# An offset of its own for every raw weight tile inside the area of cut weights

## The chip, the cores and the metric

The kernel runs on one core of one Trainium2 chip. The metric is the device time of one execution in microseconds (us). A difference of about 2% is what a measurement of this kernel is taken to tell from no change. The profiler records one execution: every instruction of the engines PE (matrix multiplies; its loads of the stationary operand are listed apart as PEld), ACT, DVE, POOL, and the queue engine SP, which issues the DMAs here.

## The reference

A bidirectional encoder trunk of two layers over 512 tokens of width 1024, all in float32. Each layer has four sub-layers:

```
for l in range(DEPTH):                                   # DEPTH = 2
    h = swiglu(rms_norm(x, norm_pre[l, 0]), ffn1_gate[l], ffn1_up[l], ffn1_down[l])   # 1024 -> 2816 -> 1024
    x = x + 0.5 * rms_norm(h, norm_post[l, 0])
    h = parallel_head_groups(rms_norm(x, norm_pre[l, 1]), ..., w_in[l], ..., w_out[l])
    x = x + rms_norm(h, norm_post[l, 1])
    h = memory_cross_attention(rms_norm(x, norm_pre[l, 2]), rms_norm(mem, mem_norm[l]), ...)
    x = x + rms_norm(h, norm_post[l, 2])
    h = swiglu(rms_norm(x, norm_pre[l, 3]), ffn2_gate[l], ffn2_up[l], ffn2_down[l])
    x = x + 0.5 * rms_norm(h, norm_post[l, 3])
```

`swiglu(u)` is `(silu(u @ w_gate) * (u @ w_up)) @ w_down`. Nearly all of the arithmetic is activations times weights that are read once from device memory.

## The kernel before

**Weights in two halves.** A float32 product is made of three products in the faster format fp32r: the weight W is cut into H (W rounded to fp32r) and L (W minus H), the activation likewise, and H·h, H·l and L·h are summed in PSUM (`mm3`, `mm3s`). So every weight goes through a pipeline of four steps, run by the class `Stream`:

1. `loader`: a DMA of 1 MB brings a raw tile (128 partitions x 2048 values) into one of two raw buffers (`RAW_BUFS`).
2. `cutter`: the raw tile is cut into chunks. ACT writes H of a chunk (a copy with rounding), DVE writes L (a subtraction). The chunks are cut strictly one after the other.
3. PE uses a chunk in its matrix multiplies.
4. `free`: after the last of them the chunk's place may be written again.

**The area of cut weights.** The chunks lie in one tile `wts` of 12,288 values (48 KB) in each partition. In the built program it starts at byte 36,800 of the partition, which is 64 bytes past a multiple of 128. A chunk of kind p or s takes 2048 values (1024 of H, then 1024 of L), a chunk of kind h takes half of that. `places` lists six places for p, at 0, 2048, ..., 10,240; five for s and one for h, which were all shifted by `SHIFT` = 16 values (64 bytes), so that s and h chunks begin at a multiple of 128 bytes. A place is taken if the bytes it covers meet no chunk that is alive (`where`), and goes to the end of its list when it is taken (`take`). Three extra chunk pairs (`wHx`, `wLx`) exist only during the transitions between sub-layers.

**Three ways of using a chunk.**

- *Plain columns* (kind c, chunks of kind p): the gate and up weights of the feed-forward layer that comes first and two column blocks of each later one, and the projections of the mixers and the attention. The chunk is the stationary operand (128 columns, 512 bytes in a row per load), the activations `uH`/`uL` stream past, 512 columns at a time (256 for the memory keys and for the first group of a sub-layer).
- *Rows* (two chunks of kind p per raw tile): `ffn_down`, `w_out`, `xattn_o`. Here the activation is stationary and the chunk streams past, 512 columns at a time. One raw tile is 48 matrix multiplies.
- *The fast form* (kind s): in three of the four feed-forward layers (`FAST`) the gate and up products are made in `gates_fast` by a Strassen-like scheme with 7 products instead of 8. DVE forms sums of weight blocks in a scratch tile `T`. One raw tile gives four chunks (three of kind s, one of kind h), used in 7 products of 12 matrix multiplies each, 84 in all, with 256 streaming columns and the chunk as the stationary operand. The products take the chunks in the order 0, 1, 0, 2, 1, 3, 3: chunk 0 is free after product 3, chunk 2 after 4, chunk 1 after 5, chunk 3 after 7. There are 54 such raw tiles, 18 in each of the three layers.

**Order.** The instructions are not written out in order: threads (the stream of weights, the cutter, evacuations of PSUM) offer operations, and `Sched` picks the next by a cost table of its own and by priorities. Where the cutter may take a place decides when its operations are offered, and so the order on ACT, DVE, SP and PE.

Of the kernel before, what the change touches and what calls it, by code (L numbers as in the profile page):

```python
# [21 lines left out]
KF = DFF // P  # L22
# [5 lines left out]
HL_BUFS = 6  # L28
# [58 lines left out]
class Op:  # L87


    def __init__(self, eng, calls, rd, wr, cost):  # L90
        self.eng, self.calls, self.rd, self.wr, self.cost = eng, calls, rd, wr, cost
        self.ready, self.size = 0.0, 0
        self.table = TABLE.get(calls[0][2].get("func")) if eng == "ACT" else None
# [267 lines left out]
class Stream:  # L361
# [6 lines left out]
    def __init__(self, k):  # L368
        self.k = k
        self.raws, self.parts, self.loaded, self.chunks = [], [], {}, {}  # L370
        self.cut = self.taken = 0
        self.limit = self.slack = 0
        self.extra = []
        self.T = None

    def open(self, raw, w):
        self.rawring = Ring(raw)
        self.w, self.live = w, set()
        self.places = {"p": [(2048 * i, 1024) for i in range(HL_BUFS)],
                       "s": [(2048 * i + self.SHIFT, 1024) for i in range(HL_BUFS - 1)],  # L380
                       "h": [(2048 * (HL_BUFS - 1) + self.SHIFT, 512)]}

    def add(self, ap, a, b, kind):
        self.parts += [(len(self.raws), j) for j in range(4 if kind == "s" else 2)]
        self.raws.append((ap, a, b, kind))

    def cols(self, w, c0, kind="c"):
        self.add(w[:, c0:c0 + 256].rearrange("(k p) c -> p k c", p=P), KD, 256, kind)
# [18 lines left out]
    def where(self, c):  # L407

        if self.extra and c < self.limit:
            return self.extra  # L410
        i, j = self.parts[c]
        kind = "p" if self.raws[i][3] != "s" else "h" if j == 2 else "s"
        for pl in self.places[kind]:
            if all(pl[0] + 2 * pl[1] <= lo or lo + 2 * n <= pl[0] for lo, n in self.live):
                return kind, pl
        return None

    def take(self, c):
        ch, got = Chunk(), self.where(c)
        if got is self.extra:  # L420
            ch.home, ch.slot = got, got.pop(0)
            return ch, ch.slot
        kind, pl = got
        self.places[kind].remove(pl)
        self.places[kind].append(pl)
        self.live.add(pl)
        ch.home, ch.slot = None, pl
        lo, n = pl
        return ch, (self.w[:, lo:lo + n], self.w[:, lo + n:lo + 2 * n])
# [54 lines left out]
class Kernel:  # L484
# [29 lines left out]
    def plan(self):  # L514

        A, st = self.D, self.st
        for l, i in self.subs:
            self.marks.append(len(st.parts))
            if i in (0, 3):
                g, u, d = (A[f"ffn{1 if i == 0 else 2}_{n}"][l] for n in ("gate", "up", "down"))  # L520
                for j in range(0, DFF, 256):
                    kind = "s" if (l, i) in FAST and j >= 256 * FAST[l, i] else "c"
                    st.cols(g, j, kind)
                    st.cols(u, j, kind)
                for k in range(0, DFF, 256):
                    st.rows(d, k)
            elif i == 1:
                w = A["w_in"][l]
                for c in (2560, 2048, 2816, 2304, 3072, 3328):
                    st.cols(w, c)  # L530
                st.block(w, 0, 1024)
                st.block(w, 512, 1024)
                for c in (0, 512, 256, 768, 1536, 1792, 3584, 3840):
                    st.cols(w, c)
                for k in range(0, D, 256):
                    st.rows(A["w_out"][l], k)
            else:
                q, k, v = (A[f"xattn_{n}"][l] for n in "qkv")
                for w, c in XORDER:
                    w = {"q": q, "k": k, "v": v}[w]  # L540
                    if w is v:
                        st.block(v, 0, c)
                        st.block(v, 512, c)
                    else:
                        st.cols(w, c)
                for k in range(0, D, 256):
                    st.rows(A["xattn_o"][l], k)
        self.marks.append(len(st.parts))


    def pool(self, name, **kw):
# [1393 lines left out]
```

## Time and profile before

| | us |
|---|---|
| median of 2 runs (2463.9 and 2466.07) | 2464.99 |
| the profiled execution, its own time | 2457.15 |
| its span, first to last instruction | 2455.4 |
| PE busy | 2406.9 (98%) |
| DVE busy | 1640.3 (67%) |
| ACT busy | 1108.3 (45%) |

The profiled execution is 7.8 us shorter than the median. Operands are named by tile: `ps<-uH,wts` is a multiply of `uH` with a chunk of `wts` into PSUM; `wts<-raw` and `wts<-T` are the cuts. A matrix multiply's recorded duration overlaps the next one's, so the pace of a stretch is its length over the number of multiplies that start in it.

### The profile page before, as it was taken

Reading aid. Unit: us, or ns where it says so; the run is one execution under the profiler, and the core shown is the slowest. Engines: PE = TensorE matmul, PEld = TensorE weight load, DVE = VectorE, ACT = ScalarE, POOL = GpSimd, SP = SyncE. Lnnn points to the kernel's source line nnn. Section 1 sums busy time; section 2 is a strip of 40 time slices with the busy share of each in tenths; the row PEclk is TensorE's granted clock in tenths of the full one; section 3 lists DMA queues with packets and bytes.
Section 4 is the critical chain, followed back from the end, with each engine's and each line's share of the span. In section 5 each row is a group of like instructions: output and inputs, shape, how many; then the busy total and the mean of one; then the engine's idle time right before and its main releaser. Section 6 shows DMA issues by size and latency. Waiting matters only on the chain. (4 is left out here: it accounts for less than half of the span.)

```text
span 2455.4 us, 37218 instructions
## 1 busy us (share of the span) xinstructions
PE 2406.9 (98%) x14990; PEld 2123.0 (86%) x14990; DVE 1640.3 (67%) x2560; ACT 1108.3 (45%) x1859; POOL 231.7 (9%) x696
## 2 busy tenths in 40 slices
PE   8999999999999999999999999998999999999998
PEld 7888888778889889998889998887888898899987
DVE  5582437768766568886378885485776665888852
ACT  4522425742444544555235554366424454455631
POOL 1000002331020020000010000125010200100001
PEclk9999999999999999999999999999999999999999
DMA  6632432355334322334213334234543243133340
GB/s 203 201 112 90 143 93 95 91 168 173 98 121 142 118 86 69 112 109 175 86 35 104 105 120 162 78 101 115 183 152 126 94 163 103 35 104 106 119 146 34
DMA packets 231202, 286.79 MB, mean 117 GB/s; under 512 B 29630, under 2 KB 190966, under 8 KB 231030
## 3 DMA queue, kind: packets, MB, share of 16 engines
q1 hardware_dynamic: 229878, 280.23, 35.3%
q10 hardware_dynamic: 1152, 4.19, 0.4%
q8 instruction: 117, 1.92, 0.3%
q14 instruction: 55, 0.45, 0.1%
HBM read 255.00 MB, written 29.39 MB: 116 GB/s over the span
## 5 line engine op out<-in xcount | busy, mean ns | idle before, releaser
L235 PE MATMUL ps<-uH,wts 128*128 128x256 f32 (+1 forms) x4064 | 994.1, 329 | 1.7 <-ACT sg L235 1.7
L235 PEld LDWEIGHTS ps<-uH,wts 128*128 128x128 f32 x4064 | 695.5, 188 | 71.1 <-ACT sg L235 1.9
L235 PE MATMUL ps<-uL,wts 128*128 128x256 f32 (+1 forms) x2032 | 665.8, 328 | 0.6 <-DVE uL L235 0.6
L235 DVE TENSOR_TENSOR wts<-raw,wts 128x1024 fp32r<-128x1024 f32 (+1 forms) x363 | 411.9, 1142 | 189.5 <-ACT wts L235 189.4
L235 ACT ACTIVATE wts<-raw 128x1024 fp32r<-128x1024 f32 (+1 forms) x363 | 357.3, 991 | 247.5 <-PE ps L235 163.0
L235 PEld LDWEIGHTS ps<-uL,wts 128*128 128x128 f32 x2032 | 386.4, 190 | 34.8 <-DVE uL L235 1.5
L235 PE MATMUL ps<-wts,uH 128*128 128x512 f32 x1152 | 363.7, 397 | 0.0
L235 PEld LDWEIGHTS ps<-wts,uH 128*128 128x128 f32 x1152 | 218.2, 191 | 44.5
L235 PE MATMUL ps<-wts,uL 128*128 128x512 f32 x576 | 227.0, 394 | 0.0
L235 ACT ACTIVATE sg<-ps 128x256 f32<-128x256 f32 (+1 forms) x196 | 93.3, 478 | 290.8 <-PE ps L235 290.7
L235 DVE TENSOR_TENSOR wts<-T,wts 128x1024 fp32r<-128x1024 f32 x108 | 132.3, 1225 | 49.2 <-ACT wts L235 48.5
L235 ACT ACTIVATE wts<-T 128x1024 fp32r<-128x1024 f32 x108 | 114.2, 1058 | 54.4 <-DVE T L235 54.4
L235 PEld LDWEIGHTS ps<-wts,uL 128*128 128x128 f32 x576 | 109.7, 191 | 23.4
L235 DVE TENSOR_TENSOR uL<-h,uH 128x512 fp32r<-128x512 f32 x76 | 51.5, 701 | 104.6 <-ACT uH L235 104.6
L235 POOL TENSOR_SCALAR sm<-sm 128x1 f32<-128x1 f32 (+1 forms) x165 | 39.2, 238 | 853.4 <-ACT junk L235 828.1
L235 ACT ACTIVATE uH<-h 128x512 fp32r<-128x512 f32 x76 | 45.6, 627 | 127.4 <-PE ps L235 123.7
L235 POOL TENSOR_SCALAR wpost<-wpost 128x1024 f32<-128x1024 f32 x4 | 15.4, 3853 | 919.1 <-DMA wpost<-in_norm_post_dram 679.8
L235 ACT ACTIVATE junk<-ps 128x512 bf16<-128x512 f32 (+1 forms) x96 | 47.1, 490 | 116.6 <-PE ps L235 102.2
L235 PE MATMUL ps<-wHx,uH 128*128 128x512 f32 x224 | 87.6, 391 | 0.0
L235 PE MATMUL ps<-wHx,uL 128*128 128x512 f32 x224 | 87.3, 390 | 0.0
L235 PE MATMUL ps<-wLx,uH 128*128 128x512 f32 x224 | 87.2, 389 | 0.0
L235 PE MATMUL ps<-s3H,wts 128*128 128x256 f32 x432 | 84.9, 281 | 0.0
(336 smaller groups left out, 4235.1 us busy)
## 6 DMA issues: line engine op xcount, KB each, us to landing
raw<-in_ffn_up_dram SPq DMA_DIRECT2D x44, 1024.0 KB, 5.1
raw<-in_ffn_down_dram SPq DMA_DIRECT2D x44, 1024.0 KB, 5.0
raw<-in_ffn_gate_dram SPq DMA_DIRECT2D x43, 1024.0 KB, 5.1
raw<-in_w_in_dram SPq DMA_DIRECT2D x32, 1024.0 KB, 6.1
raw<-in_w_out_dram SPq DMA_DIRECT2D x8, 1024.0 KB, 6.0
raw<-in_xattn_q_dram SPq DMA_DIRECT2D x8, 1024.0 KB, 5.3
raw<-in_xattn_k_dram SPq DMA_DIRECT2D x8, 1024.0 KB, 5.2
raw<-in_xattn_v_dram SPq DMA_DIRECT2D x8, 1024.0 KB, 5.1
```

The lines of the kernel that those rows point to most:

```text
L235: fn(*a, **kw)
```

## The change

Each raw tile gets a shift of its own, in values of 4 bytes, by which all of its chunks lie further on in the area. The 64-byte shift of the s and h places goes out of the list of places and into the shifts' default.

```diff
-                       "s": [(2048 * i + self.SHIFT, 1024) for i in range(HL_BUFS - 1)],
-                       "h": [(2048 * (HL_BUFS - 1) + self.SHIFT, 512)]}
+                       "s": [(2048 * i, 1024) for i in range(HL_BUFS - 1)],
+                       "h": [(2048 * (HL_BUFS - 1), 512)]}
...
+        self.shifts.append(self.SHIFT if kind == "s" else 0)
...
-        for pl in self.places[kind]:
-            if all(pl[0] + 2 * pl[1] <= lo or lo + 2 * n <= pl[0] for lo, n in self.live):
-                return kind, pl
+        for q in self.places[kind]:
+            pl = (q[0] + self.shifts[i], q[1])
+            if pl[0] + 2 * pl[1] <= 2048 * HL_BUFS and all(pl[0] + 2 * pl[1] <= lo or lo + 2 * n <= pl[0] for lo, n in self.live):
+                return kind, q, pl
...
+        fast = [i for i, r in enumerate(st.raws) if r[3] == "s"]
+        cols = [i for i, r in enumerate(st.raws) if 4 <= i < KF]
+        rows = [i for i, r in enumerate(st.raws) if r[1] == 2]
+        fine = list(range(1, 16))
+        for some, sh in ((fast, [0] + fine + [16 * k + d for k in range(1, 8) for d in (0, 4, 8, 12)] + [144, 160, 192, 224, 256, 320, 384, 448, 512, 640]),
+                         (cols, fine[::2] + [24, 32, 48, 64, 72, 80, 96, 112, 116, 120]),
+                         (rows, fine + [16 * k + d for k in range(1, 8) for d in (0, 4, 8, 12)])):
+            for i, e in zip(some, sh):
+                st.shifts[i] = e
```

All 54 fast raw tiles get a shift from the list: 0; 1 to 15; every fourth value from 16 to 124; and ten from 144 to 640. Counted from the start of the partition, a shift of 16 (and of 48, 80, 112, 144) starts a tile at a multiple of 128 bytes, as all fast tiles did before; 13 of the others (0 among them) start at an odd multiple of 64 bytes, 36 at no multiple of 64 bytes. 18 plain column tiles of the first feed-forward layer get shifts of 1 to 120 (the first eight of them odd), and the first 43 row tiles get 1 to 15 and every fourth value from 16 to 124, of which 36 are no multiple of 16 values; a chunk that the cutter puts into an extra pair takes no shift, so 52 row chunks are shifted inside the area, 43 of them by no multiple of 16 values. All other tiles lie where they lay.

Each instruction is still there, with the same shape and the same count on every engine. Two things besides the addresses are different. A chunk with a shift covers the end of its place and the beginning of the next one, so it shuts out a chunk with another shift from that neighbour; and a p chunk with a shift no longer fits in the sixth place, which ends with the area. In the fast form, three to five chunks were alive when a new one was placed, now three or four. And since the cutter takes places at other moments, the order on the engines differs.

On DVE, in the middle of the second fast layer, the work on one raw tile stood like this before (`T<-raw` forms the sums, the `wts` rows write L, `sg` and `h` are the evacuation of finished products):

```order
L235 TENSOR_TENSOR T_10296<-raw_83 128x2x512 [waits DMAHW7_49,DVE_49]
L235 TENSOR_TENSOR T_10296<-raw_83,T_10296 128x512 [waits DVE_49]
L235 TENSOR_TENSOR wts<-raw_83,wts 128x1024 [waits Activation_49]
L235 TENSOR_TENSOR wts<-T_10296,wts 128x1024 [waits PE_49,Activation_49]
L235 TENSOR_TENSOR wts<-raw_83,wts 128x512 [waits PE_49,Activation_49]
L235 TENSOR_TENSOR T_10296<-raw_83,T_10296 128x512 [waits DVE_49]
L235 TENSOR_TENSOR sg_10299<-ps_76,sg_10299 128x512
L235 TENSOR_TENSOR sg_10299<-ps_77,sg_10299 128x512 [waits PE_49]
L235 TENSOR_TENSOR wts<-T_10296,wts 128x1024 [waits Activation_49]
```

The same raw tile now:

```order
L235 TENSOR_TENSOR T_10296<-raw_83 128x2x512 [waits DMAHW7_49,DVE_49]
L235 TENSOR_TENSOR T_10296<-raw_83,T_10296 128x512 [waits DVE_49]
L235 TENSOR_TENSOR wts<-raw_83,wts 128x1024 [waits PE_49,Activation_49]
L235 TENSOR_TENSOR h_10284<-sg_10299,sg_10297 128x512
L235 TENSOR_TENSOR wts<-T_10296,wts 128x1024 [waits PE_49,Activation_49]
L235 TENSOR_TENSOR sg_10298<-ps_81,sg_10298 128x512 [waits Activation_49]
L235 TENSOR_TENSOR wts<-raw_83,wts 128x512 [waits Activation_49]
L235 TENSOR_TENSOR T_10296<-raw_83,T_10296 128x512 [waits DVE_49]
L235 TENSOR_TENSOR sg_10298<-ps_78,sg_10298 128x512 [waits PE_49]
L235 TENSOR_TENSOR wts<-T_10296,wts 128x1024 [waits Activation_49]
```

The L of chunk 0 now waits for PE as well as for ACT, since its place is that of the raw tile before, and evacuations have moved in between the cuts of chunks 0, 1 and 2.

On ACT, at the same place, before (from the copy of PSUM that follows the raw tile's first two products):

```order
L235 ACTIVATE sg_10299<-ps_76 128x512 [waits PE_49]
L235 ACTIVATE wts<-T_10296 128x1024 [waits DVE_49]
L235 ACTIVATE wts<-raw_83 128x1024 [waits DMAHW7_49]
L235 ACTIVATE sg_10299<-ps_76 128x256 [waits PE_49]
L235 ACTIVATE wts<-T_10296 128x1024 [waits DVE_49,Activation_49]
L235 ACTIVATE sg_10299<-ps_76 128x256 [waits PE_49]
L235 ACTIVATE wts<-raw_83 128x512 [waits Activation_49]
```

And now:

```order
L235 ACTIVATE wts<-T_10296 128x1024 [waits DVE_49]
L235 ACTIVATE sg_10298<-ps_81 128x512 [waits PE_49]
L235 ACTIVATE wts<-raw_83 128x1024 [waits DMAHW7_49]
L235 ACTIVATE sg_10298<-ps_81 128x256 [waits PE_49]
L235 ACTIVATE wts<-T_10296 128x1024 [waits DVE_49,Activation_49]
L235 ACTIVATE sg_10298<-ps_81 128x256 [waits PE_49]
L235 ACTIVATE wts<-raw_83 128x512 [waits Activation_49]
```

Here only the H of the previous raw tile's last chunk has moved ahead of the first copy of PSUM; the H of chunk 0 still follows that copy, and the H of chunk 1 the second one.

More of the change, by code (lines that the diff above doesn't have):

```diff
@@ L370, in __init__ @@
         self.raws, self.parts, self.loaded, self.chunks = [], [], {}, {}
+        self.shifts = []
         self.cut = self.taken = 0
@@ L422, in take @@
             return ch, ch.slot
-        kind, pl = got
-        self.places[kind].remove(pl)
-        self.places[kind].append(pl)
+        kind, q, pl = got
+        self.places[kind].remove(q)
+        self.places[kind].append(q)
         self.live.add(pl)
```

## The prediction

> **What bounds the kernel now.** I read the page first, then the waits of PE, then the pace of PE in stretches of one kind, since the change moves addresses that PE reads.
>
> ```profile
> span 2455.4 us, 37218 instructions
> ...
> PE 2406.9 (98%) x14990; PEld 2123.0 (86%) x14990; DVE 1640.3 (67%) x2560; ACT 1108.3 (45%) x1859; POOL 231.7 (9%) x696
> ...
> PE   8999999999999999999999999998999999999998
> ...
> PEclk9999999999999999999999999999999999999999
> ```
>
> PE is busy for 98% of the span at a granted clock that never drops, in every slice. It waits for little:
>
> ```profile
> engine line waited for: us in total, times, longest us
> PE ps L235 <- DVE tmp L235: 17.4, 9, 8.8
> PE ps L235 <- DVE Vt L235: 10.6, 2, 5.3
> ...
> PE ps L235 <- DVE wLx L235: 0.2, 1, 0.2
> ```
>
> The two largest waits are for normalized activations (`tmp`) and for the recurrent mixer (`Vt`). For a cut weight it waits 0.2 us in all. So the time is the number of matrix multiplies times their pace, and a change of addresses can cost in two ways: a multiply takes longer, or a chunk comes late because it finds no place.
>
> The pace, by stretches of one kind (columns: length; PE busy with the multiplies that touch the stretch; loads of the stationary operand; DVE; ACT; POOL; clock; DMA):
>
> ```profile
> 80.00:370.00 290.00, 290.00 (x1281) 240.26 (x1280) 143.56 (x180) 95.91 (x117) 6.08 (x15) 1.00 0.37 124
> 960.00:1112.00 152.00, 152.00 (x1293) 152.00 (x1292) 130.87 (x156) 80.35 (x115) 0.00 (x0) 1.00 0.32 105
> 784.00:793.00 9.00, 9.00 (x77) 9.00 (x77) 7.67 (x11) 5.99 (x14) 0.00 (x0) 1.00 0.39 137
> 681.00:715.00 34.00, 33.94 (x149) 27.70 (x149) 20.25 (x35) 15.79 (x29) 4.46 (x19) 1.00 0.62 217
> ```
> ```profile
> 1992.00:2000.50 8.50, 8.50 (x73) 1.00 0.46 136
> ```
> ```profile
> L235 PE MATMUL ps<-s1H,wts 128*128 128x256 f32 x432 | 84.8, 281 | 0.0
> L235 PEld LDWEIGHTS ps<-s1H,wts 128*128 128x128 f32 x432 | 69.6, 188 | 0.0
> L235 PE MATMUL ps<-mH,wts 128*128 128x256 f32 x256 | 47.0, 283 | 0.0
> L235 PEld LDWEIGHTS ps<-mH,wts 128*128 128x128 f32 x256 | 40.4, 192 | 0.1
> L235 PE MATMUL ps<-wts,hxH 128*128 128x512 f32 x192 | 59.5, 391 | 2.0 <-ACT hxH L235 2.0
> ```
>
> A multiply of 256 columns lasts 281 ns, so about 2.4 of those counted began before the stretch; of 512 columns (391 ns) about 1.7.
>
> - Fast form (960 to 1112): 152.00 / (1293 - 2.4) = 117.8 ns each. Its chunks begin at a multiple of 128 bytes. The loads of the stationary operand fill the whole stretch, 152.00 of 152.00.
> - Memory keys (784 to 793 and 1992 to 2000.5), the same size of multiply: 9.00 / 74.6 = 120.6 and 8.50 / 70.6 = 120.4. Their chunks begin 64 bytes past a multiple of 128. The load takes 192 instead of 188 ns and the multiply 283 instead of 281.
> - 512 columns, first feed-forward layer (80 to 370): 290.00 / 1279.3 = 226.7. The loads leave 50 of 290 us free.
> - 512 columns with another stationary tile, in `w_out` (681 to 715): 33.94 / 147.3 = 230.4. So 3.7 ns per multiply is the largest difference of pace between these stretches at equal size.
>
> The reader should see that where the loads have no gap, a start 64 bytes off goes with 2.7 ns per multiply (120.5 - 117.8), and that the fast form stands on the better side of it.
>
> **The change part by part.** *Instructions:* none is added or removed on PE, DVE, ACT, POOL or SP, the DMAs are the same 1 MB each, and no queue is passed by a step that issues more than before. Cost 0.
>
> *Fast form, addresses.* 54 raw tiles x 84 = 4536 multiplies. Five raw tiles keep a multiple of 128 bytes, 13 get an odd multiple of 64, 36 no multiple of 64. For the 13 the row of the memory keys is the price: 13 x 84 x 2.7 ns = 2.9 us. For the 36 no row of PE has weights at such a start. From above I bound them by 3.7 ns (11.2 us); from below by the pace at which 256 columns stream, half of the 226.7 of 512 columns, 113.4, which would be a gain of 4.4 ns (13.3 us less; over all 4536 multiplies 20 us less). I take 2.7 ns, as for the 13, since the load at an odd start also runs across one boundary more than an even one: 36 x 84 x 2.7 = 8.2 us. All of it lies on the path that sets the end, for PE has no pause there. Together 11.1 us.
>
> *Rows.* 43 chunks of 24 multiplies have a start that is no multiple of 64 bytes, as the streaming operand: 1032 multiplies. Bounds 0 (the other operand decides the pace) and 3.7 ns (3.8 us); I take 2.7 ns, 2.8 us. *Plain columns* with a shift: the chunk is the stationary operand of 512-column multiplies, whose loads have 50 of 290 us to spare; 0, hidden by the stream of the activations; if that cover were gone, 36 chunks x 24 x 2.7 ns = 2.3 us.
>
> *Cuts.* ACT and DVE write and read at odd starts now. The convolution already does that: `xp` is written by ACT two values (8 bytes) after its start, and read by DVE from 0, 1, 3 and 4 values on. The second and fourth rows are aligned neighbours of the same size:
>
> ```profile
> L235 DVE SCALAR_TENSOR_TENSOR cv<-xp,cwT,cv x96: 741/752/1851, 412.9 to 1684.0; 128x512 f32<-128x512 f32 x96
> L235 ACT ACTIVATE xp<-ps x24: 577/582/602, 410.8 to 1675.4; 128x512 f32<-128x512 f32 x24
> ```
> ```profile
> L235 DVE SCALAR_TENSOR_TENSOR x<-tmp,sm,x 128x512 f32<-128x512 f32 x64 | 45.8, 749 | 54.4 <-POOL sm L235 54.1
> L235 ACT ACTIVATE sg<-ps 128x512 f32<-128x512 f32 x88 | 52.0, 595 | 140.7 <-PE ps L235 140.6
> ```
>
> 752 at the median against 749, and 582 against 595: no price. Cost 0; what would hide a small one is DVE's free time, 21 of 152 us in the fast stretch.
>
> *Places.* This is where a wait could arise. In the fast form a chunk mostly takes over the place of the same chunk of the raw tile before. Counted in the order of products, chunk 1 is free after product 5 and needed again in product 2 of the next raw tile: 3 products, 36 multiplies, 4.24 us (it was 96 multiplies, 11.3 us). Chunk 0 has 48 multiplies or 5.65 us (in ten cases 36), chunk 3 has 60 or 7.07, chunk 2 has 72 or 8.48 as before. In that room must fit, for chunk 1:
>
> ```profile
> L235 ACT ACTIVATE sg<-ps 128x256 f32<-128x256 f32 x31 | 11.9, 384 | 47.1 <-PE ps L235 47.1
> ...
> L235 ACT ACTIVATE wts<-T 128x1024 fp32r<-128x1024 f32 x31 | 32.8, 1057 | 11.4 <-DVE T L235 11.4
> ...
> L235 DVE TENSOR_TENSOR wts<-T,wts 128x1024 fp32r<-128x1024 f32 x31 | 38.0, 1226 | 15.8 <-ACT wts L235 15.6
> ```
> ```profile
> 1056.72 1.05 ACT L235 ACTIVATE wts<-T 128x1024 fp32r<-128x1024 f32 x1
> ...
> 1057.81 1.22 DVE L235 TENSOR_TENSOR wts<-T,wts 128x1024 fp32r<-128x1024 f32 x1 [1.39 <-ACT wts L235]
> ```
>
> The copy of PSUM that stands ahead of it on ACT (384), H (1057), L (1226): 2.67 us, with 0.04 between H and L in the timeline. That leaves 1.5 us. Behind the waiting L on DVE stand the evacuations `sg` and `h`; DVE works 130.87 of 152 us, so 8.5 of the 9.9 us that a raw tile takes (84 x 117.8 ns), and has 1.4 us per raw tile to wait in. I take 0. Bounds: 0, and 1 us for each of 54 raw tiles, 54 us (DVE's spare time used up and chunk 1 late by the next cut in its queue, 1.2 us); it is nearer to 0, since the sum of the chain is 1.5 us inside its room. In the plain columns four chunks fit instead of six, three or more of 24 x 226.7 ns = 5.4 us ahead of PE, against a cut of about 2.3 us: 0. *Order:* other waits of PE move with it; 28 us of them stand in the rows above, and I take 0 within 5 us either way.
>
> *Sum:* 11.1 + 2.8 = 13.9 us on the profiled execution's 2457.15: 2471. The median of the runs is 7.8 us above that execution, and the time that is asked for is a median, so 2464.99 + 13.9 = 2479 us.
>
> [...]
>
> **The rivals.**
>
> 1. *Hidden.* The pace of the fast form is set by the stream and not by the load; the difference to the memory keys has another cause, such as their moving tile. For it: in one stretch the activations are `s1` to `s3` and `uH`, in the other `mH`. Against it: load and multiply are both longer there, 192 and 283. Then all terms are 0: 2465 us. [...]
> 2. *A gain.* Some starts are better than the present one, up to the stream's 113.4: 2465 - 20 = 2445 us at the very most. Against it: all 54 raw tiles would have to profit.
> 3. *Places* (the other side, slower). DVE runs behind in the fast form, and the L of chunk 1 comes after PE wants it. For it: PE waits on every piece of this chain, and the room falls from 11.3 to 4.24 us. Against it: the chain needs 2.67. It decides when it costs (49.3 - 13.9) / 54 = 0.66 us per raw tile, that is when L comes 1.5 + 0.66 = 2.2 us later than the chain says. At 1 us: 2465 + 14 + 54 = 2533 us.
> 4. *Half rate at fine starts.* PE reads the 12 fast raw tiles whose start is no multiple of 16 bytes at half its pace: 12 x 84 x 117.8 ns = 119 us more, 2584 us, and rows would add to it. For it: no row shows PE reading at such a start. Against it: DVE and ACT do so at no price (752 and 582 above). [...] No run here shows PE at it yet.
>
> **How the numbers follow.** The forecast as summed (2470 to 2495) has a chance of 0.50, for its main price is a row of the same multiply; hidden 0.25; gain 0.05; places 0.10; half rate 0.10. The range reaches from the gain's end, 2446, to 2512, where the forecast's upper bounds end (14 as summed; 5 more if all 49 fast raw tiles and the row chunks pay 3.7 instead of 2.7 ns; 2 for the columns; 5 for the order; and 21 for chunks late by 0.4 us on each of 54 raw tiles): it leaves out rivals 3 and 4, 0.20. A measurement of this kernel tells about 2%, 49 us, from no change: faster 0.01, same 0.79, slower 0.20.
>
> **What would show it.** In the changed kernel's profile a stretch inside the fast form, such as 40 us in the second of its three layers, would show a pace of 120 to 121 ns with PE's waits for `wts` still under 5 us in all; rows of `ffn_down` would stay under 231 ns. Hidden: 117.8 everywhere. Places: PE waiting for `DVE wts`, several tens of us. Half rate: the first 15 raw tiles of the first fast layer at twice the pace, and loads well over 192 ns. The forecast is wrong if the pace differs strongly between tiles that differ by one value in their start, or if the first feed-forward layer, where loads have room, grows by more than 5 us.

## The result, and the profile after

The changed kernel takes 2517.93 us at the median (two runs, 2515.67 and 2520.19) against 2464.99: a ratio of 1.0226, 95% interval 1.0207 to 1.0245. It is slower by more than the 2% that count as a difference, and 6 us beyond the upper end of the range.

From the page of the changed kernel (2515.67 us is this execution's own time), the span, PE's busy time with its share, and the granted clock by slices:

```profile
span 2513.9 us, 37245 instructions
...
PE 2443.1 (97%) x14990; PEld 2146.5 (85%) x14990; DVE 1638.8 (65%) x2560; ACT 1099.9 (44%) x1855; POOL 235.9 (9%) x696
...
PEclk9999999999999999999999999999999999999999
```

The span grew by 58.5 us. PE is busy for 36 us more with the same 14,990 multiplies, so part of the loss is multiplies that last longer, and 22 us (58.5 - 36.2) are pauses. DVE and ACT do not work longer. (ACT carries out four instructions fewer, 1855 instead of 1859: four table loads that the changed order saves. All other work is the same in number.)

The clock row hides something: 9 stands for 90% or more, and a slice lasts 63 us. It hid it in the kernel before as well, whose granted clock was at 0.50 in five stretches of 3.4 to 6.8 us, 24 us in all, and once more at its end. One of them begins in a pause of 5.29 us for `Vt`; the first microsecond behind that pause in the kernel before:

```profile
474.80:475.80 1.00, 1.00 (x3) 0.61 (x3) 1.00 (x2) 0.17 (x1) 0.00 (x0) 0.50 0.00 0
```

The waits of PE say where to look:

```profile
engine line waited for: us in total, times, longest us
PE ps L235 <- DVE tmp L235: 40.3, 9, 8.9
...
PE ps L235 <- DVE wts L235: 4.0, 4, 1.0
```

The wait for `tmp`, the normalized activations that open a sub-layer, went from 17.4 to 40.3 us. The wait for cut weights is small, 4.0 us. Five of the nine waits for `tmp` are new pauses of over 5 us, each at a change of sub-layer: at 404.9, 752.1, 926.2, 1291.4 and 1652.5 us. Here is the second of them in stretches (columns as in the prediction: length; busy time of PE, PEld, DVE, ACT, POOL with the number of instructions; granted clock; DMA), first of the changed kernel, then the same place of the kernel before:

```profile
748.00:752.00 4.00, 4.00 (x35) 3.87 (x33) 3.83 (x9) 1.04 (x3) 0.00 (x0) 1.00 0.39 136
752.10:757.20 5.10, 0.03 (x1) 0.03 (x1) 2.03 (x4) 0.55 (x2) 2.58 (x13) 0.95 0.61 206
757.20:763.00 5.80, 5.66 (x24) 5.12 (x25) 1.96 (x3) 1.19 (x2) 0.00 (x0) 0.50 0.00 0
763.20:773.00 9.80, 9.80 (x82) 9.80 (x81) 4.30 (x5) 4.21 (x6) 0.00 (x0) 0.98 0.23 76
```
```profile
738.20:739.40 1.20, 0.30 (x3) 0.07 (x1) 0.74 (x2) 0.99 (x2) 0.35 (x2) 1.00 0.00 0
739.40:745.00 5.60, 5.43 (x46) 5.23 (x47) 5.34 (x8) 2.14 (x3) 0.00 (x0) 1.00 0.03 7
```

Before, PE paused for about 1 us, and the next 5.6 us held 46 multiplies at full clock. Now it pauses for 5.1 us, and the 5.8 us after that hold 24 at a granted clock of 0.50. So one such place is paid twice: with the pause, and with half of the time that the clock stays down after it. The five pauses are 28.1 us together, where they were 4.6 us before, and the clock stays down for 4.8 to 6.3 us after each, 28.7 us together. As an estimate from these figures that is 23.5 us of pauses and 14.3 us of multiplies at half pace, 38 us. The five changes are those in front of which the row tiles have shifts; at the last two changes of sub-layer, which follow row tiles without a shift, there is no such pause.

What makes `tmp` late stands in DVE's timeline (start, length, operation; `x<-tmp` adds the finished half of a token tile to the residual stream, `tmp<-x` writes the normalized tile that PE transposes). The kernel before:

```profile
731.23 2.08 DVE L235 SCALAR_TENSOR_TENSOR x<-tmp,sm,x 128x512 f32<-128x512 f32 x3
733.22 1.22 DVE L235 TENSOR_TENSOR wts<-raw,wts 128x1024 fp32r<-128x1024 f32 x1
...
736.35 1.42 DVE L235 SCALAR_TENSOR_TENSOR tmp<-x,sm,wpre 128x512 f32<-128x512 f32 x2
738.66 1.41 DVE L235 SCALAR_TENSOR_TENSOR tmp<-x,sm,wpre 128x512 f32<-128x512 f32 x2 [0.90 <-POOL sm L235]
```

The changed kernel:

```profile
743.30 0.75 DVE L235 SCALAR_TENSOR_TENSOR x<-tmp,sm,x 128x512 f32<-128x512 f32 x1
743.97 1.22 DVE L235 TENSOR_TENSOR wts<-raw,wts 128x1024 fp32r<-128x1024 f32 x1
745.10 0.75 DVE L235 SCALAR_TENSOR_TENSOR x<-tmp,sm,x 128x512 f32<-128x512 f32 x1
745.77 1.22 DVE L235 TENSOR_TENSOR wts<-raw,wts 128x1024 fp32r<-128x1024 f32 x1
...
748.88 1.42 DVE L235 SCALAR_TENSOR_TENSOR tmp<-x,sm,wpre 128x512 f32<-128x512 f32 x2
750.21 0.75 DVE L235 SCALAR_TENSOR_TENSOR x<-tmp,sm,x 128x512 f32<-128x512 f32 x1
750.88 1.22 DVE L235 TENSOR_TENSOR wts<-raw,wts 128x1024 fp32r<-128x1024 f32 x1
...
756.37 1.42 DVE L235 SCALAR_TENSOR_TENSOR tmp<-x,sm,wpre 128x512 f32<-128x512 f32 x2 [3.07 <-POOL sm L235]
```

Two token tiles are in flight. Before, their three `x<-tmp` stand together, so that the small steps of the two norms run side by side on DVE and POOL. Now a cut follows each `x<-tmp`, and the third `x<-tmp` comes only after the whole norm of the other tile. Its own norm then runs alone on POOL, while DVE and PE wait for it. From the first `x<-tmp` to the last `tmp<-x` it is 13.07 us now (756.37 - 743.30) and was 7.43 (738.66 - 731.23).

The cuts stand there because of the planner's rule `Stream.prio`: the urgency of a cut is (0, 1, 30, 60) by the number of chunks cut and not yet taken, and the norms of the token tiles have the priorities (-1, -1, 13, -1). With two chunks in hand a cut (30) comes after every norm; with one or none (1 or 0) it comes ahead of the norm with priority 13, which is the last to end. The planner counts by its own clock, but the two traces bear it out: at the five places, when the first of these `x<-tmp` begins, two chunks were cut and not yet used before the change, and one or none after it. Three to five cuts then stand ahead of the last `tmp<-x`, where one stood.

For the whole span, the times from each multiply with cut weights to PE's next instruction, summed by kind (us, worked out from the two traces; ns in brackets: the mean of those without a pause):

| | before | after | difference |
|---|---|---|---|
| first groups of sub-layers and memory keys, 256 columns | 237.2 (119.7) | 278.2 (119.9) | +41.0 |
| fast form, 256 columns | 536.2 (117.2) | 548.9 (119.2) | +12.7 |
| rows | 754.7 (227.3) | 760.0 (229.7) | +5.3 |
| other plain columns, 512 columns | 609.2 (227.4) | 609.6 (229.1) | +0.4 |

All other multiplies together take 1.0 us less. The first line is the changes of sub-layer; its pace is what it was, so its 41 us are pauses and multiplies at half clock. In the other three lines the pace is longer; rows and plain columns win back a part of it in shorter pauses.

### The profile page after: what moved, and what is told of

It reads as the page before. It is cut to its first block, busy times and chain, and to the rows that moved or that the text cites. A ratio compares the mean times of both kernels' runs of the same rounds, so it can differ in the third digit from the quotient of the medians.

```text
span 2513.9 us, 37245 instructions
## 1 busy us (share of the span) xinstructions
PE 2443.1 (97%) x14990; PEld 2146.5 (85%) x14990; DVE 1638.8 (65%) x2560; ACT 1099.9 (44%) x1855; POOL 235.9 (9%) x696
## 4 chain that ended last, share of the span: by engine, by line
PE 84%; DVE 6%; POOL 4%; issue 2%; ACT 2%; DMA 2%; SPq 0%; DVEq 0%; ACTq 0%; POOLq 0%
PE ps L235 84%; POOL sm L235 3%; DVE rt L235 1%; DVE tmp L235 1%; ACT junk L235 1%; POOL ts L235 1%; DVE uL L235 1%; DVE wts L235 1%; DVE x L235 1%; DMA k<-qkd 0%; DVE X L235 0%; ACT uH L235 0%; DMA raw<-in_w_in_dram 0%; DMA rvd<-rt 0%; DVE sm L235 0%
## 5 line engine op out<-in xcount | busy, mean ns | idle before, releaser
L235 PE MATMUL ps<-uH,wts 128*128 128x256 f32 (+1 forms) x4288 | 1049.2, 330 | 0.8 <-ACT cv L235 0.8
L235 PEld LDWEIGHTS ps<-uH,wts 128*128 128x128 f32 x4288 | 739.4, 191 | 74.1 <-issue 1.2
L235 PE MATMUL ps<-uL,wts 128*128 128x256 f32 (+1 forms) x2144 | 704.4, 329 | 2.7 <-DVE uL L235 1.8
L235 DVE TENSOR_TENSOR wts<-raw,wts 128x1024 fp32r<-128x1024 f32 x358 | 408.2, 1146 | 257.8 <-ACT wts L235 203.4
L235 ACT ACTIVATE wts<-raw 128x1024 fp32r<-128x1024 f32 x358 | 352.1, 990 | 246.3 <-PE ps L235 187.9
L235 PE MATMUL ps<-wts,uH 128*128 128x512 f32 x1024 | 322.7, 396 | 0.0
L235 PEld LDWEIGHTS ps<-wts,uH 128*128 128x128 f32 x1024 | 191.8, 189 | 41.9 <-issue 0.3
L235 PE MATMUL ps<-wts,uL 128*128 128x512 f32 x512 | 202.0, 395 | 0.0
L235 DVE TENSOR_TENSOR wts<-T,wts 128x1024 fp32r<-128x1024 f32 x108 | 132.3, 1225 | 65.1 <-ACT wts L235 64.6
L235 ACT ACTIVATE wts<-T 128x1024 fp32r<-128x1024 f32 x108 | 114.2, 1058 | 46.4 <-DVE T L235 46.1
L235 PE MATMUL ps<-wHx,uH 128*128 128x512 f32 x288 | 113.0, 392 | 0.0
L235 PE MATMUL ps<-s1H,wts 128*128 128x256 f32 x432 | 87.1, 284 | 4.0 <-DVE wts L235 4.0
```

What stands on the lines that cost most here:

```text
L235: fn(*a, **kw)
```

## The experiments

Theory A: the places that the offsets cost leave fewer chunks in hand when a sub-layer ends; cuts then go ahead of the last norm; PE pauses and its clock is halved. Against it stand: the new start addresses themselves (B), chunks that are late (D, I), and that the paces have nothing to do with starts (C, F, H). The kernel before was run beside each: 2462.96 us at the median for the first four experiments, 2460.53 for the next four, 2461.76 for the last two. Only `e6_urgent1` is slower by clearly more than 2%; the interval of `e1_places` reaches across that line. The smaller differences are read from their intervals and from the paces in the traces.

**Lost places without new starts** (`e1_places`). A place is taken only if it is free at its shifted address, as in the changed kernel, and at its old one; the chunk is written and read at the old one.

```diff
...
-                return kind, q, pl
+            at = q[0] + (0 if kind == "p" else self.SHIFT)
+            m = 2 * q[1]
+            if pl[0] + m <= 2048 * HL_BUFS and all((pl[0] + m <= lo or lo + 2 * n <= pl[0]) and (at + m <= r or r + 2 * n <= at)
+                                                   for lo, n, r in self.live):
+                return kind, q, (pl[0], q[1], at)
...
-        lo, n = pl
+        _, n, lo = pl
```

> Bookkeeping of the places as in the changed kernel (a place is taken only if it is free at its shifted and at its old address), but the chunks are written and read at the old addresses: lost places and the order that follows, no new start. Theory A (fewer chunks cut ahead when a sub-layer ends, so cuts stand in front of the last norm chain on DVE, TensorE pauses 5 us or more and its granted clock falls): 2495 to 2520 us, with 4 or more pauses of over 5 us before transposes of tmp and as many stretches at clock 0.5. Rival B (the new start addresses cost the time): within 5 us of the kernel before, 2460 to 2470, no new pauses.

Measured: 2508.14 us, ratio 1.0189 (1.0174 to 1.0204). Six pauses of 5.1 to 7.0 us before transposes of `tmp`, each with the clock at 0.50 behind it. The fast form's pace is that of before (117.8 ns in all 54 tiles), rows 227.3, columns 227.3. PE's waits:

```profile
PE ps L235 <- DVE tmp L235: 46.1, 9, 8.4
...
PE ps L235 <- DVE wts L235: 0.3, 1, 0.3
```

So lost places alone cost 45 us, with no chunk at a new address and 0.3 us of waits for a chunk. Theory B falls as the main cause.

**Starts without lost places** (`e2_addr`). The order of the instructions on every engine is that of the kernel before. The places lie 64 bytes further apart, and each raw tile's chunks are moved by its shift modulo 16 inside them.

```diff
-        lo, n = pl
+        n = pl[1]
+        lo = pl[0] // 2048 * 2064 + self.shifts.get(self.parts[c][0], 0)
...
-                     wp.tile([P, HL_BUFS * 2048], F32R, name="wts"))
+                     wp.tile([P, HL_BUFS * 2064], F32R, name="wts"))
...
-        self.junkt = cp.tile([P, 512], BF16, name="junk")
+        self.junkt = cp.tile([P, 512], mybir.dt.int8, name="junk")
```

> The new starts alone: same order of every instruction as the kernel before, each raw tile's chunks at an offset of 0 to 15 elements of its own within places that are 64 bytes further apart; a scratch tile of the sums of squares is 1 byte an element instead of 2 to make room. Theory A: only the paces change, fast form about +9, plain columns +4, rows +8 us at most: 2470 to 2490, no new pauses. Rival B (addresses cost all of it): 2505 to 2525. Rival C (starts cost nothing, the pace differences come from the order): 2462 to 2468.

Measured: 2486.03 us, ratio 1.0099 (1.0084 to 1.0114), PE's wait for `tmp` 18.7 us. Paces: fast form 118.3 ns, columns 231.3, rows 232.2. So starts cost too, but by pace only, and here more in rows (+16 us) and columns (+9) than in the fast form (+4). The offsets are not those of the changed kernel: every second place begins 64 bytes off for all plain chunks, and that has a price of its own (in `p16` columns went from 227.4 to 233.3 ns).

**The rule alone, taken out of the changed kernel** (`e3_prio`). Until all input features of a sub-layer are there, a cut ranks behind every norm.

```diff
-        return (0, 1, 30, 60)[max(0, min(self.cut - self.taken + self.slack, 3))]
+        p = (0, 1, 30, 60)[max(0, min(self.cut - self.taken + self.slack, 3))]
+        return p if all(self.k.feats) else max(p, 14)
```

> The changed kernel with one rule altered: until all of a sub-layer's input features are there, a cut never goes ahead of a norm chain. Theory A: cuts no longer stand before the last chain's multiplies on DVE, the pauses of 5 to 7 us and the stretches at half clock go, 30 to 40 us come back: 2478 to 2490. Rival D (the chunks themselves are late for want of places, so the wait only turns from tmp to wts): 2508 to 2525.

Measured: 2480.49 us, ratio 1.0077 (1.0062 to 1.0092), so 1.5% of the 2.3% are gone, 37 us. DVE's timeline at the same change of sub-layer, and PE's waits:

```profile
735.77 2.08 DVE L235 SCALAR_TENSOR_TENSOR x<-tmp,sm,x 128x512 f32<-128x512 f32 x3
737.76 1.22 DVE L235 TENSOR_TENSOR wts<-raw,wts 128x1024 fp32r<-128x1024 f32 x1
...
740.89 1.42 DVE L235 SCALAR_TENSOR_TENSOR tmp<-x,sm,wpre 128x512 f32<-128x512 f32 x2
743.22 1.41 DVE L235 SCALAR_TENSOR_TENSOR tmp<-x,sm,wpre 128x512 f32<-128x512 f32 x2 [0.91 <-POOL sm L235]
```
```profile
PE ps L235 <- DVE tmp L235: 16.7, 9, 8.7
...
PE ps L235 <- DVE wts L235: 3.9, 4, 1.0
PE ps L235 <- DVE wLx L235: 2.8, 2, 2.6
```

The three `x<-tmp` are together again, 7.45 us from the first to the last `tmp<-x`, and the wait for `tmp` is 16.7 us. Of the five new pauses none is left; one of 2.57 us for a late chunk (`wLx`) has come. The places are as few as in the changed kernel, and the waits for chunks are 6.7 us (3.9 and 2.8) where the changed kernel has 4.0, so the wait has not turned from `tmp` to chunks: D falls. The first line of the table above would read 245.0 us here, 33 less than in the changed kernel. What is left, 18 us over the kernel before, is about what the paces give: 118.4 ns in the fast form, 229.6 in rows and 229.1 in columns, together 17 us.

**The rule alone, put into the kernel before** (`e6_urgent1`). Places and starts are untouched.

```diff
-        return (0, 1, 30, 60)[max(0, min(self.cut - self.taken + self.slack, 3))]
+        return (0, 1, 30, 60)[max(0, min(self.cut - self.taken + self.slack - (0 if all(self.k.feats) else 1), 3))]
```

> The kernel before, its places and starts untouched; while a sub-layer's input features are still coming, the cutter is given the urgency it would have with one chunk less in hand. In DVE's order 3 or 4 cuts then stand inside the last norm chain of 7 changes of sub-layer, where the kernel before has 1. Theory A: 5 to 7 pauses of 5 to 7 us before tmp's transposes, each followed by a stretch at clock 0.5, +35 to +55 us: 2496 to 2518. Rival I (the cuts ahead are no matter, TensorE waits because chunks are missing): no longer than before, 2455 to 2468, since chunks are cut earlier here.

Measured: 2520.93 us, ratio 1.0234 (1.021 to 1.0259), the loss of the whole change and a little over the expected range. Seven pauses of 5.12 to 6.17 us before transposes of `tmp`, and three of 3.66 to 5.86 us elsewhere (before multiplies that wait for `gl` and `sg`). The first groups of the sub-layers and the memory keys take 291.9 us in its trace, instead of 237.2. The timeline shows the order of the changed kernel, 13.05 us from the first `x<-tmp` to the last `tmp<-x`:

```profile
746.33 0.75 DVE L235 SCALAR_TENSOR_TENSOR x<-tmp,sm,x 128x512 f32<-128x512 f32 x1
747.00 1.22 DVE L235 TENSOR_TENSOR wts<-raw,wts 128x1024 fp32r<-128x1024 f32 x1
748.13 0.74 DVE L235 SCALAR_TENSOR_TENSOR x<-tmp,sm,x 128x512 f32<-128x512 f32 x1
748.80 1.22 DVE L235 TENSOR_TENSOR wts<-raw,wts 128x1024 fp32r<-128x1024 f32 x1
...
753.33 0.74 DVE L235 SCALAR_TENSOR_TENSOR x<-tmp,sm,x 128x512 f32<-128x512 f32 x1
...
759.38 1.42 DVE L235 SCALAR_TENSOR_TENSOR tmp<-x,sm,wpre 128x512 f32<-128x512 f32 x2 [2.97 <-POOL sm L235]
```

At all seven places two chunks were in hand when the first of these `x<-tmp` began, as before the change, and PE waits 0.3 us for `wts`, so chunks were not short: I falls, and the order on DVE is shown to be the cause.

**Lost places with the altered rule** (`e5_places_prio`): the edits of `e1_places` and `e3_prio` together.

> Lost places without new starts (the first experiment) together with the altered rule of the cuts. Theory A (lost places cost only by way of cuts that stand ahead of the last norm chain): back to within 10 us of the kernel before, 2460 to 2473, pauses of over 5 us before tmp's transposes no more than before. Rival D (fewer places also make chunks late): 2480 or more, with waits for wts or wLx.

Measured: 2450.51 us, ratio 0.9956 (0.994 to 0.9972): below the range, 10 us less than the kernel before.

```profile
PE ps L235 <- DVE tmp L235: 17.5, 11, 8.6
PE ps L235 <- DMA k<-qkd: 6.6, 2, 3.7
```

Behind the start no pause of over 3.8 us is left. So lost places as such cost nothing; they cost only through the rule. Where the gain over the kernel before comes from was not separated, and the altered rule was not run in the kernel before, so that it may have a small gain of its own there too: the wait for `Vt` (10.6 us before) is not in its list of waits, and 16 fast tiles ran at 113.3 to 115.9 ns instead of 117.8.

**All fast tiles at one other start** (`s7`, `SHIFT = 7`; `s13n`, `SHIFT = 13`). In `s13n` the planner's table rounds the starts down to 16, so that the order stays that of the kernel before; in `s7` only PE's and POOL's order is the same, DVE's and ACT's differ in places:

```diff
-    SHIFT = 16
+    SHIFT = 13
...
-        p0, f0 = divmod(ap.offset, pitch)
+        p0, f0 = divmod(ap.offset, pitch); f0 -= f0 % GRAIN if t.name.startswith("wts") else 0
```

> The kernel before with all fast tiles at start 7 instead of 16, one number changed. In the changed kernel the three fast tiles at starts 7, 8 and 9 ran at 133 ns a matmul, the others at 113 to 122. Theory E (the start sets the pace): all 4,116 multiplies of the fast form at 133 instead of 117 ns, +60 to +70 us: 2525 to 2535. Rival F (the pace has levels that the start alone does not choose): 2455 to 2480, with tiles of one start at more than one pace.

Measured: 2459.6 us, ratio 0.9991 (0.9981 to 1.0). E falls: all 54 tiles at this start, 4536 multiplies, ran at 116.7 ns (one at 116.9), not 133. In `e3_prio`, where the starts are those of the changed kernel, the tiles at starts 7, 8 and 9 ran at 116.7, 118.4 and 119.9 ns. Stretches of the changed kernel (in its eighth fast tile, at start 7, and its eleventh, at start 10), of `e3_prio` (its eighth fast tile), and of `s7`, with 78, 86, 79 and 1287 multiplies:

```profile
1043.00:1053.00 10.00, 10.00 (x78) 10.00 (x77) 7.57 (x10) 5.35 (x7) 0.00 (x0) 1.00 0.32 105
1077.00:1087.00 10.00, 10.00 (x86) 10.00 (x86) 9.64 (x12) 4.85 (x7) 0.00 (x0) 1.00 0.33 105
```
```profile
1020.00:1029.00 9.00, 9.00 (x79) 9.00 (x78) 7.60 (x10) 5.00 (x8) 0.00 (x0) 1.00 0.38 117
```
```profile
960.00:1110.00 150.00, 150.00 (x1287) 150.00 (x1286) 131.69 (x155) 81.33 (x116) 0.00 (x0) 1.00 0.34 106
```

> The kernel before with all fast tiles at start 13 instead of 16, order kept as before. The tile at this start took 113.7 ns a multiply in the changed kernel, whatever the rule of the cuts. Theory G: 4536 x 3.5 ns = 16 us less, 2444 to 2450, so faster than both kernels. Rival F (levels that the start alone does not choose): 2452 to 2475, tiles of this one start at more than one pace.

Measured: 2463.99 us, ratio 1.0017 (1.0003 to 1.0032). G falls: one start, two paces in one run. The first and the third fast layer ran at 120.0 ns, the second at 113.3, all at full clock:

```profile
960.00:1110.00 150.00, 150.00 (x1252) 150.00 (x1251) 127.02 (x149) 78.01 (x110) 0.00 (x0) 1.00 0.34 106
1310.00:1410.00 100.00, 100.00 (x883) 99.96 (x883) 88.45 (x104) 55.01 (x79) 0.00 (x0) 1.00 0.34 106
```

**The kernel before, again** (`b2`).

> The kernel before, once more, for its profile alone. There, six fast tiles in a row (numbers 107 to 112) ran at 113.3 ns a multiply and the other 48 at 117.8, all at one start. Rival J (place in the program decides): the same six again. Theory K (a state of the pipeline that a disturbance sets and that lasts until the next): other tiles, or none; in either case 113.3, 116.7, 117.8 or 120 over whole tiles.

Measured: one time of 2460.35 us. J holds: the same six tiles at 113.3 ns, the same two at 115.9 and 115.8 where it changes inside a tile, 117.8 in the rest. Stretches inside the six and behind them:

```profile
1300.00:1350.00 50.00, 50.00 (x441) 49.95 (x441) 43.91 (x52) 26.07 (x37) 0.00 (x0) 1.00 0.38 119
1366.00:1416.00 50.00, 50.00 (x427) 49.98 (x426) 43.77 (x52) 27.93 (x41) 0.00 (x0) 1.00 0.37 114
```

The pace is thus fixed by the program, and not by the start of the chunk alone.

**All plain chunks moved** (`p16`, by 64 bytes; `p8n`, by 32 bytes with the rounding of `s13n`). The order is that of the kernel before.

```diff
-        lo, n = pl
+        lo, n = pl[0] + (16 if kind == "p" else 0), pl[1]
...
-                     wp.tile([P, HL_BUFS * 2048], F32R, name="wts"))
+                     wp.tile([P, HL_BUFS * 2048 + 16], F32R, name="wts"))
```

> The kernel before with every plain chunk 64 bytes (16 elements) further on, nothing else moved: same order, same places, same 128 partitions. In the changed kernel plain chunks at this offset ran at 230.6 ns (columns) and 230.0 (rows), unmoved ones at 227.8 and 227.6. Theory G (the start sets the pace): 2592 x 2.8 ns + 3263 x 2.4 ns = 15 us, 2474 to 2482. Rival H (those paces came from the order of the work or from neighbours): 2459 to 2467.

Measured: 2467.31 us, ratio 1.0024 (1.0014 to 1.0035), at the edge of H's expectation and below G's. Columns went from 227.4 to 233.3 ns, more than G had it, rows only to 228.8, and the fast form, whose chunks were not moved, got faster, 117.2 to 116.2. The longer area moves tiles behind it by 64 bytes (`s1H` to `s3L` and `mH` among them), so this run moved one operand of the fast form and of the memory keys also. `uH` and `uL`, which the columns stream, lie at the same bytes in the built programs, so in the columns the chunk is the only operand that moved. The memory keys, whose chunks now begin at a multiple of 128 bytes, still take 120.0 ns.

> As before, but every plain chunk 32 bytes (8 elements) further on; the planner's table of what depends on what rounds the starts down, so that the order stays that of the kernel before. In the changed kernel chunks at this offset ran at 233.1 ns (columns) and 233.8 (rows). Theory G: 2592 x 5.3 ns + 3263 x 6.2 ns = 34 us, 2490 to 2502. Rival H: 2459 to 2467.

Measured: 2478.22 us, ratio 1.0069 (1.0049 to 1.0089): H falls, and G's size was twice too large. Columns 233.3 ns, as in `p16`; rows at this start 233.2, where `p16` has 228.8. Between these two runs only the chunks' starts differ. The first layer's columns (they end at 262 us before, at 268 here) in the kernel before, in `p16` and in `p8n`:

```profile
80.00:260.00 180.00, 180.00 (x796) 149.12 (x795) 99.30 (x132) 61.28 (x69) 0.00 (x0) 1.00 0.39 131
```
```profile
80.00:260.00 180.00, 180.00 (x773) 144.48 (x772) 96.95 (x128) 58.41 (x64) 0.00 (x0) 1.00 0.38 123
```
```profile
80.00:260.00 180.00, 180.00 (x773) 144.92 (x772) 96.87 (x128) 58.51 (x64) 0.00 (x0) 1.00 0.37 123
```

A uniform move of all plain chunks makes the columns slower by 2.6%, with the loads still leaving 35 of 180 us free. So the start of a chunk does count; but 32 and 64 bytes give the same pace in columns and not in rows.

## Why the prediction was wrong

**The step that failed** is the end of *Places* with *Order*: "In the plain columns four chunks fit instead of six, three or more of 24 x 226.7 ns = 5.4 us ahead of PE, against a cut of about 2.3 us: 0", and for the order "0 within 5 us". Both asked only whether a chunk comes late for PE, and looked at the fast form and the columns, not at the rows, which end a sub-layer and lose places as well. A chunk hardly comes late: waits for cut weights rose from 0.2 to 4.0 us. But fewer chunks in hand raise the cutter's rank in the planner, and its cuts then delay another chain on DVE, that of the last norm. This term is +41 us in the first groups of the sub-layers, confirmed from both sides: the rule taken out of the changed kernel gives back 37 us, and the rule alone put into the kernel before costs 59. The half clock behind each pause belongs to the term; the prediction read the clock row as a clock "that never drops, in every slice", and the trace before has it at 0.50 behind pauses of 5.29 us. The 17.4 us wait for `tmp`, quoted as the largest wait of PE, was the place to look at: it names the chain with no slack, and the question would have been what can now stand ahead of it on its engines.

**The fast form's addresses** were put at 11.1 us. The pace rose from 117.2 to 119.2 ns, 9.2 us over 4536 multiplies; another 3.5 us are four pauses for a chunk. The size was nearly right by luck, the reason was not right: 3.9 us of the 9.2 are three tiles at 133.3 ns, which `e3_prio` ran at 116.7 to 119.9 from the same starts. Nor does a run show a price of one boundary more, by which the 36 tiles were given their 2.7 ns: they ran at 113.7 to 133.3 ns. A start at a multiple of 128 bytes is not the better side: tiles at such a start ran at 113.3 and at 117.8 ns in one run (`b2`), and tiles 116 bytes past one at 113.3 and at 120.0 (`s13n`). The 2.7 ns by which the memory keys are slower are not the price of the 64 bytes either: in `p16` their chunks begin at a multiple of 128 bytes, and they take 120.0 ns as before (there `mH` lies 64 bytes further too).

**Rows and plain columns** were sized at 2.8 and 0 us and came to 7.6 and 4.5 by pace (3263 x 2.33 ns and 2592 x 1.72 ns). The cover named for the columns, 50 of 290 us free of loads, does not hide it: in `p8n` the loads still leave 35 of 180 us free, and the pace is 233.3 instead of 227.4. (The stretch from 80 to 370 us, which the prediction took for columns, holds rows from 262 us on; the columns alone have 31 of 180 us free.) In the changed kernel the tiles whose start is no multiple of 64 bytes ran at 230 to 235 ns in columns and at 230 to 237 in rows. With `e1_places`, which has the old starts and ran at 117.8, 227.3 and 227.3, the starts are shown to carry these paces.

**Cuts** at no price is confirmed. The subtraction that writes L in the fast form takes 1225 ns before and after, the copy that writes H 1058 ns before and after:

```profile
L235 DVE TENSOR_TENSOR wts<-T,wts 128x1024 fp32r<-128x1024 f32 x108 | 132.3, 1225 | 65.1 <-ACT wts L235 64.6
L235 ACT ACTIVATE wts<-T 128x1024 fp32r<-128x1024 f32 x108 | 114.2, 1058 | 46.4 <-DVE T L235 46.1
```

**The rivals.** *Hidden* is out: paces of all three kinds moved. *Gain*: single tiles did run at 113.4 to 113.7 ns, but not all. *Places* had the right word and the wrong place: its mechanism, chunk 1 late in the fast form, cost 3.5 us in four pauses. *Half rate* is out: the slowest tiles took 133.3 ns, the other tiles at starts 1 to 15 between 113.7 and 121.9.

Of what the profile was to show, the wait for `wts` under 5 us came; the second fast layer ran at 118.3 ns, not at 120 to 121, and shifted rows of `ffn_down` at 231 to 237 ns in the first layer, not under 231. Both signs of being wrong came too: tiles that differ by one value in their start ran at 121.9 and 133.3 ns (starts 6 and 7), and the first feed-forward layer grew by 7.0 us, 4.6 of them in its columns. It named no sign for the changes of sub-layer, where most of the time went.

## What stays open

What chooses a multiply's pace among 113.3, 116.7, 117.8, 120.0 and 133.3 ns was not settled. It was the same in `b2` as in the kernel before, it can change inside a tile at full clock (in the kernel before from 117.8 to 113.3 ns at 1296.6 us and back at 1363.8 us), and in `s13n` the same starts of both operands in the built program, but for whole multiples of 8 KB in the chunk's place, gave 113.3 and 120.0. The starts of the activations count as well: in `p16` and `p8n` the order and the fast form's chunks are those of the kernel before, of its operands only `s1H` to `s3L` have moved, and its pace is 116.2 instead of 117.2. By which rule they count stays open. Nor was the price of the halved clock measured apart from the pauses; the sum of the two is.

## What to carry to other kernels

When a change takes room from a stream of prefetched work, ask not only whether the stream runs dry but what its rising urgency pushes aside: follow the chain with the largest wait through every engine that it shares with the stream. Where an order is made by a planner, a comparison of the two orders at the changes of phase shows such a displacement before any run; here three to five cuts stood inside the last norm chain where one had stood. And a price that one pair of stretches shows (2.7 ns, aligned against not aligned) needs a second pair before it is called the price of the thing in which the pair was seen to differ.

## What the runs showed of the hardware

- Each of the 39 pauses of PE of 3.66 us or more behind the start of the kernel, in the twelve profiles of this case, had a granted clock of 0.50 at its end or within 2 us of it, and full clock was back 3 to 7 us after the pause. So had 15 of the 18 between 2.05 and 3.3 us, and none of the 11 between 1.5 and 2.02 us; but one of 1.48 us had it (`e6_urgent1`, ending at 693.2 us), so length alone does not decide. A pause of 5.1 us thus brings some 3 us more in multiplies at half pace (an estimate: half of the 6.3 us at 0.50 behind it), which no wait shows.
- The clock also fell to 0.50 where PE did not pause, in or just behind runs of 32x32 multiplies: in the kernel before at 1809.75 us for 3.41 us, in the changed kernel at 609.9 and 1852.3 us for 6.83 us each.
- In the traces of the kernel before and of the changed kernel the stretches at 0.50 last 3.41 us (four of them) or 6.83 us (nine), but for the one in each that the end of the kernel cuts off. Such a stretch also followed a pause of 2.06 us in `e5_places_prio`, from 1295.4 us on, before a multiply of `uH` with a chunk (0.50 until 1300.9 us).
- PE read chunks that start 1 to 15 values of 4 bytes into their places, and not at half rate: in the changed kernel fast tiles at these starts ran at 113.7 to 133.3 ns, against 117.8 at one start before, and rows at starts that are no multiple of 64 bytes at 230 to 237 ns, against 227.3.
- The pace of 256-column multiplies at full clock was the same over many tiles: 117.8 ns in most of the kernel before and 113.3 in six of its tiles, 116.7 in `s7`, 120.0 in two of the three fast layers of `s13n`, 133.3 in three tiles of the changed kernel. In `b2`, the kernel before run again, the same six tiles ran at 113.3 ns and most others at 117.8.
- Multiplies of fp32r operands are the faster ones in the kernel before: of 512 columns, one of `uH` with a chunk (fp32r) lasts 394 ns in the record, one of `q` with `k` (float32) 601.
